# Softmax denominators of a hybrid encoder layer: from a repeated reciprocal out of PSUM to a copy, a trip through DRAM and a compact reciprocal

## Chip, cores and metric

The kernel runs on one core of a Trainium2 chip. The metric is the device time of one execution in microseconds; the time given for a kernel is the median of its runs. Engines are named as in the profile: PE is TensorE's matmul, PEld its weight load, DVE is VectorE, ACT ScalarE, POOL GpSimd, SP SyncE, which issues nearly all DMAs here.

## The reference

One encoder layer with two attention branches side by side, run on two groups of requests, 2048 and 512 tokens of width 1024. Cut to what matters:

```python
proj = h @ w_in                       # h: adaLN-modulated RMSNorm of x
qa, ka, va, za, cq, ckv, kr, zb, gm = jnp.split(proj, IN_SPLITS, axis=-1)
ya = windowed_gqa(qa, ka, va, sink) * jax.nn.silu(za)     # branch A
yb = mla(cq, ckv, kr, g_q, w_uq, g_kv, w_ukv) * jax.nn.silu(zb)   # branch B
ga, gb = jnp.split(jax.nn.sigmoid(gm), 2, axis=-1)
merged = ga * (ya @ w_oa) + gb * (yb @ w_ob)
out = x + gate_res[:, None, :] * (merged @ w_out)         # then a final RMSNorm

def attend(q_blk):                    # inside mla, 8 heads of 64 values
    s = jnp.einsum("bqhd,bkhd->bhqk", q_blk, k).astype(jnp.float32)
    p = jax.nn.softmax(s, axis=-1).astype(v.dtype)
    return jnp.einsum("bhqk,bkhd->bqhd", p, v)
```

The change concerns the division in mla's softmax: one denominator per head and token, 8 x 512 of them per chunk of 512 tokens.

## The kernel before

The 2560 tokens are five chunks of T = 512: c = 0 to 3 are the long request, c = 4 the short one. The kernel has three stages: the input projections; mla's scores, exponentials and value products; and a last stage that runs from 1311 us to the end. Every fp32 matmul of a projection is done as three passes (`mm3`, L99 to 102) over operands split into a high and a low part; each weight tile of 128x1024 is loaded by SP (`wload`, L109), its high part cast by ACT (L122) and its low part subtracted by POOL (L123).

The stage in the middle leaves, per chunk, unnormalised outputs of mla in DRAM (`o_d`) and partial sums of the exponentials over 128 partitions (`sm_d`). The last stage then does, chunk by chunk: the denominators (`inv_den`, L888 to 901), branch B's gate path (`zb(1)`, tiles z_1_0 to z_1_3), the merge gates (gm, two tiles of 24 matmuls for each of eight j) with branch B's projection (po, `branch_out`), the next chunk's `inv_den`, branch A's gate path (`zb(0)`), its projection, and the output projection (out). Branch A's windowed attention is done in groups (`attn_group`, L136 to 198, a block of 128 tokens and four heads each) set between the others.

`inv_den(c)` has two halves, b = 0 and 1. In each, PE sums the partial sums of four heads with a matmul by a matrix of ones that has 32 columns (L896), so the 512 denominators of one head stand in PSUM on 32 partitions, all alike: a 128x512 tile `den`, of which 4 rows differ. DVE inverts all of it into the SBUF tile `rd` (L899), and SP stores one row of each head to DRAM (`rd_d`, L901). `inv_den(0)` stands ahead of the loop over chunks; `inv_den(c + 1)` stands in chunk c, ahead of `zb(0)`. In `zb(1)` SP loads each head's row back, spread over 64 partitions (`dn`, L919), POOL adds the two halves of the output (`ob`, L920), and DVE multiplies by `dn` (L921). The gate path's z then goes through tanh (L928), DVE (`zt`, L929, which is what frees z's PSUM bank), POOL (L930) and a split into Y (L932, L933).

What sets the order: the middle stage's order is written out by hand; the last stage is ordered by the framework's scheduler, which works from its own simulated timeline, so a changed instruction can move others on every engine. Each engine then runs its instructions in that order. Buffers: PSUM tag "a" (den, z, gm, po, out) has four banks, used in turn, so z_1_2 takes the bank of den_0 and z_1_3 that of den_1; `rd` has one buffer in SBUF, so the second half of `inv_den` waits until the first half's rows have landed; split weights have three load buffers. SP's DMAs use eight completion semaphores in turn, so a DMA can wait for the one issued eight before it.

In `attn_group` the chain is: scores `as` (PE, L165, L166), mask and maximum (DVE, L168), `ncol` and `ecol` (DVE, L171, L172), exponentials (ACT, L173, L175), `dcol` and `rcol` (DVE, L177, L178), the scaling of S by rcol (DVE, L180), transposes `pT` (PE, L186), the split into PT (ACT L188, DVE L189), and the value product `aa` (PE, L190, L191).

```python
dn = p3.tile([P, T], F32, name=f"rd{c}_{b}", tag="rd", bufs=1)
nc.vector.reciprocal(out=dn, in_=ps)
for i in range(4):
    nc.sync.dma_start(rd_d[c][4 * b + i:4 * b + i + 1], dn[32 * i:32 * i + 1])
```

Of the kernel before, what the change touches and what calls it, by code (L numbers as in the profile page):

```python
# [9 lines left out]
F32 = mybir.dt.float32  # L10
# [8 lines left out]
P = 128  # L19
D = 1024  # L20
KD = D // P
T = 512
NS = 4
NC = 5
HA = 8
HB = 8
# [12 lines left out]
def encoder(ctx: ExitStack, tc: tile.TileContext, x_prompt, x_sample, c_prompt, c_sample, b_ada, g_norm, g_q,  # L39
            w_uq, g_kv, w_ukv, sink, g_final, t_mod, t_gate, t_col, t_a, t_b, t_oa, t_ob, t_out, rope_c, rope_s, bias, sel, y_prompt, y_sample):  # L40
    nc = tc.nc
# [12 lines left out]
    dram = ctx.enter_context(tc.tile_pool(name="dram", bufs=1, space=DRAM))  # L54
# [5 lines left out]
    def pa(name):  # L60
        return pps["a"].tile([P, 512], F32, name=name, tag="a")
# [25 lines left out]
    o_d = [dram.tile([2, HB * 64, T], F32, name=f"o_d{c}") for c in range(NC)]  # L87
    sm_d = [dram.tile([HB, P, T], F32, name=f"sm_d{c}") for c in range(NC)]
    rd_d = [dram.tile([HB, T], F32, name=f"rd_d{c}") for c in range(NC)]
    rw_d = [dram.tile([HB, 4, P], F32, name=f"rw_d{c}") for c in range(NC)]  # L90
    gate_d = dram.tile([2, D], F32, name="gate_d")
    ones_d = dram.tile([P, 1024], F32, name="ones_d")
# [13 lines left out]
    def wload(tp, nm, loads, nr, tag="wr"):  # L106
        wr = tp.tile([P, 1024], F32, name=f"wr{nm}", tag=tag, bufs=nr)
        for dst, src in loads:
            issue["w"].dma_start(dst(wr), src)  # L109
        return wr  # L110
# [749 lines left out]
    with psum("ps3a", 4) as pps["a"], psum("ps3t", 1) as pps["t"], psum("ps3c", 1) as pps["c"], pool("p3c") as p3c, pool("p3y") as p3y, pool("p3l") as p3, \  # L860
# [28 lines left out]
        def inv_den(c):  # L889
            for b in range(2):  # L890
                ps = pa(f"den{c}_{b}")
                w = [wload(p3r, f"sm{c}_{b}_{j}", [(lambda t: t.rearrange("p (h n) -> p h n", n=T),
                                                    sm_d[c][j:j + 2].rearrange("h p n -> p h n"))], NR)
                     for j in (4 * b, 4 * b + 2)]
                for i in range(4):
                    nc.tensor.matmul(ps[32 * i:32 * i + 32, :], ones, w[i // 2][:, i % 2 * T:(i % 2 + 1) * T],  # L896
                                     start=True, stop=True)
                dn = p3.tile([P, T], F32, name=f"rd{c}_{b}", tag="rd", bufs=1)
                nc.vector.reciprocal(out=dn, in_=ps)  # L899
                for i in range(4):  # L900
                    nc.sync.dma_start(rd_d[c][4 * b + i:4 * b + i + 1], dn[32 * i:32 * i + 1])  # L901

        inv_den(0)
        H = H0
        for c in range(NC):
# [64 lines left out]
            if c + 1 < NC:  # L970
                inv_den(c + 1)
# [140 lines left out]
```

## Time and profile before

| What | Value |
|---|---|
| Runs | 2640.05, 2640.7 and 2644.24 us; median 2640.7 |
| Profiled execution | 2639.86 us |
| Span of its profile, first to last instruction | 2638.1 us |
| Mean granted TensorE clock | 0.991 of full speed |
| Last stage | from about 1311 us to the end |

The rows below come from the one profiled execution. A row of a timeline gives the start in us from the span's start, the duration in us, the engine, the line, the operation with out<-in, the shape and type, a count where several are taken together, and in brackets the idle time of the engine just before and what ended it. SPq is SP issuing a DMA: its duration is the issue, not the transfer. A row of the waits gives the engine and line that waited, what it waited for, the us in total, the times and the longest. Ends of matmuls are modelled, so the pace of PE is read from starts.

### The profile page before, as it was taken

The numbers are of one execution on the slowest core, as the hardware profiler recorded it, in microseconds if no ns is written. First come the engines' busy times: TensorE is split into PE (matmuls) and PEld (weight loads), VectorE is DVE, ScalarE is ACT, GpSimd is POOL, SyncE is SP. The second block draws the span as 40 slices with busy tenths as digits, with TensorE's granted clock in tenths as the row PEclk, the third lists the DMA queues.
The fourth block names the chain that finished last, engine by engine and source line by source line (L and its number), as shares of the span: only waits on it lengthen the run. The fifth ranks groups of instructions, "written<-read, shape, count | busy, mean of one in ns | idle before, by whom it ended". The sixth has DMA issues, their size and how long they took to land. (4 is left out here: it accounts for less than half of the span.)

```text
span 2638.1 us, 33977 instructions
## 1 busy us (share of the span) xinstructions
PE 2555.9 (97%) x11842; PEld 2037.5 (77%) x11842; DVE 1689.0 (64%) x2511; ACT 1325.1 (50%) x2105; POOL 1597.4 (61%) x992
## 2 busy tenths in 40 slices
PE   7999999899999999999999999999999999999998
PEld 4888888767777777776777777877887788778876
DVE  3654644579999999999764567446644663466325
ACT  3554543367777777777644443434343434344432
POOL 2564554278888888887852376337733773377355
PEclk8999999999999999999999999999999999999999
DMA  8677765563232232222264445345544453445341
GB/s 307 217 239 239 242 214 181 154 191 92 55 96 75 60 87 75 71 68 83 80 212 161 157 167 196 121 151 174 188 135 143 165 188 124 162 150 199 107 169 53
DMA packets 199431, 392.34 MB, mean 149 GB/s; under 512 B 18086, under 2 KB 97383, under 8 KB 197658
## 3 DMA queue, kind: packets, MB, share of 16 engines
q1 hardware_dynamic: 186210, 353.32, 41.7%
q10 hardware_dynamic: 13050, 36.86, 4.4%
q8 instruction: 93, 1.52, 0.2%
q14 instruction: 78, 0.64, 0.1%
HBM read 286.52 MB, written 103.58 MB: 148 GB/s over the span
## 5 line engine op out<-in xcount | busy, mean ns | idle before, releaser
L736 POOL TENSOR_TENSOR pl<-pf,ph 128x1024 fp32r<-128x1024 f32 x272 | 655.8, 2414 | 135.6 <-ACT pf L729 135.3
L123 POOL TENSOR_TENSOR wlgm<-wrgm,whgm 128x1024 fp32r<-128x1024 f32 x80 | 196.3, 2457 | 326.5 <-ACT whgm L122 283.1
L728 ACT ACTIVATE ph<-s 128x1024 fp32r<-128x1024 f32 x272 | 278.6, 1024 | 182.2 <-PE s L721 180.7
L687 DVE TENSOR_REDUCE mx<-mp 128x1 f32<-128x1024 f32 x240 | 292.7, 1219 | 38.5 <-PE mp L681 36.7
L749 DVE TENSOR_TENSOR ac<-ac,pf 128x512 f32<-128x512 f32 x424 | 294.2, 694 | 21.3 <-ACT pf L729 14.8
L729 ACT ACTIVATE pf<-s 128x1024 f32<-128x1024 f32 x272 | 275.7, 1014 | 0.0
L101 PE MATMUL gm<-H,wlgm 128*128 128x512 f32 x640 | 252.2, 395 | 0.0
L100 PE MATMUL gm<-H,whgm 128*128 128x512 f32 x640 | 250.2, 395 | 0.9 <-ACT whgm L122 0.9
L102 PE MATMUL gm<-H,whgm 128*128 128x512 f32 x640 | 250.7, 393 | 0.0
L719 PE MATMUL s<-Q,K 97*128 97x512 f32 x544 | 216.1, 397 | 3.6 <-DMA Q<-qr_d 3.6
L720 PE MATMUL s<-Q,K 96*128 96x512 f32 x544 | 215.8, 397 | 0.0
L721 PE MATMUL s<-Q,K 96*128 96x512 f32 x544 | 215.1, 395 | 0.0
L761 PE MATMUL a<-ph,V 128*128 128x512 f32 x544 | 175.3, 403 | 0.0
L764 PE MATMUL a<-pl,V 128*64 128x512 f32 x544 | 169.7, 393 | 0.5 <-POOL pl L736 0.4
L681 PE MATMUL mp<-K,Q 96*128 96x512 f32 x512 | 163.5, 400 | 5.9 <-DVE mx L687 3.7
L123 POOL TENSOR_TENSOR wlz<-wrz,whz 128x1024 fp32r<-128x1024 f32 x39 | 95.2, 2448 | 119.5 <-ACT whz L122 112.5
L168 DVE CUSTOM_DVE_ANT_0 S<-as,mask,snk 128x384 f32<-128x384 f32 (+1 forms) x160 | 89.2, 585 | 99.4 <-PE as L166 67.3
L189 DVE TENSOR_TENSOR PT<-pT,PT 128x512 fp32r<-128x512 f32 x112 | 77.0, 688 | 110.4 <-ACT PT L188 108.8
L100 PEld LDWEIGHTS gm<-H,whgm 128*128 128x128 f32 x640 | 119.4, 188 | 26.3 <-issue 1.7
L102 PEld LDWEIGHTS gm<-H,whgm 128*128 128x128 f32 x640 | 120.4, 188 | 23.7
L101 PEld LDWEIGHTS gm<-H,wlgm 128*128 128x128 f32 x640 | 120.3, 188 | 23.4
L100 PE MATMUL z<-H,whz 128*128 128x512 f32 x320 | 127.0, 397 | 8.5 <-DVE rd L899 4.4
(254 smaller groups left out, 6487.9 us busy)
## 6 DMA issues: line engine op xcount, KB each, us to landing
wrgm<-in_t_col_dram SPq DMA_DIRECT2D x80, 512.0 KB
wrz<-in_t_col_dram SPq DMA_DIRECT2D x40, 512.0 KB
wrw<-in_t_out_dram SPq DMA_DIRECT2D x40, 512.0 KB
wrqa<-in_t_col_dram ACTq DMA_DIRECT2D x20, 512.0 KB
qa_d<-qa SPq DMA_DIRECT2D x40, 256.0 KB
k_d<-kn SPq DMA_DIRECT2D x20, 512.0 KB
qn_d<-qn SPq DMA_DIRECT2D x20, 512.0 KB
v_d<-vt SPq DMA_DIRECT2D x20, 512.0 KB
```

Source lines behind the costliest of these rows:

```text
L100: nc.tensor.matmul(ps, wh, mh, start=first, stop=False)
L101: nc.tensor.matmul(ps, wl, mh, start=False, stop=False)
L102: nc.tensor.matmul(ps, wh, ml, start=False, stop=last)
L123: (eng or nc.gpsimd).tensor_tensor(out=wl[:, :n], in0=wr[:, :n], in1=f(wh[:, :n]), op=ALU.subtract)
L687: nc.vector.tensor_reduce(out=it.mx[:, i // 2, i % 2:i % 2 + 1], in_=it.mp.rearrange("p a b -> p (a b)"), axis=AX.X, op=ALU.max)
L719: nc.tensor.matmul(ps[:, j, :], K[0:97, 0, ks], Q[0:97, 0, :], start=True, stop=False)
L720: nc.tensor.matmul(ps[:, j, :], K[0:96, 1, ks], Q[0:96, 0, :], start=False, stop=False)
L721: nc.tensor.matmul(ps[:, j, :], K[0:96, 0, ks], Q[0:96, 1, :], start=False, stop=True)
L728: nc.scalar.activation(ph, it.s, AF.Exp)
L729: nc.scalar.activation(pf, it.s, AF.Exp)
L736: nc.gpsimd.tensor_tensor(out=pl, in0=it.pf[p], in1=f(it.ph[p]), op=ALU.subtract)
L749: nc.vector.tensor_tensor(out=sm if last and j else it.acc, in0=it.acc, in1=pf[:, j], op=ALU.add)
```

## The change

ACT, not DVE, empties the PSUM tile of each half of `inv_den`: a copy into `rd` (L900 of the new kernel). SP stores the four differing rows, still not inverted, to a new DRAM buffer `dd_d` (L902). After both halves SP loads all 8 x 512 denominators of the chunk as 128 partitions by 32 columns (`dc`, L905), DVE inverts those (`rc`, L906), and SP stores them to `rd_d` (L907). The loads of `dn` are as before. Lines move by 1 after L90 and by 6 after `inv_den`: `dn` is L925 now, `ob` times `dn` L927, `zt` L935, the scaling of S L181, pT L187, the weight cast L123.

```diff
--- before.py
+++ after.py
@@ -87,6 +87,7 @@
     o_d = [dram.tile([2, HB * 64, T], F32, name=f"o_d{c}") for c in range(NC)]
     sm_d = [dram.tile([HB, P, T], F32, name=f"sm_d{c}") for c in range(NC)]
     rd_d = [dram.tile([HB, T], F32, name=f"rd_d{c}") for c in range(NC)]
+    dd_d = [dram.tile([HB, T], F32, name=f"dd_d{c}") for c in range(NC)]
     rw_d = [dram.tile([HB, 4, P], F32, name=f"rw_d{c}") for c in range(NC)]
     gate_d = dram.tile([2, D], F32, name="gate_d")
     ones_d = dram.tile([P, 1024], F32, name="ones_d")
@@ -896,9 +897,14 @@
                     nc.tensor.matmul(ps[32 * i:32 * i + 32, :], ones, w[i // 2][:, i % 2 * T:(i % 2 + 1) * T],
                                      start=True, stop=True)
                 dn = p3.tile([P, T], F32, name=f"rd{c}_{b}", tag="rd", bufs=1)
-                nc.vector.reciprocal(out=dn, in_=ps)
+                nc.scalar.copy(dn, ps)
                 for i in range(4):
-                    nc.sync.dma_start(rd_d[c][4 * b + i:4 * b + i + 1], dn[32 * i:32 * i + 1])
+                    nc.sync.dma_start(dd_d[c][4 * b + i:4 * b + i + 1], dn[32 * i:32 * i + 1])
+            dc = p3.tile([P, 32], F32, name=f"dc{c}", tag="dc", bufs=2)
+            rc = p3.tile([P, 32], F32, name=f"rc{c}", tag="dc", bufs=2)
+            nc.sync.dma_start(dc, dd_d[c].rearrange("h (a b) -> (h a) b", b=32))
+            nc.vector.reciprocal(out=rc, in_=dc)
+            nc.sync.dma_start(rd_d[c].rearrange("h (a b) -> (h a) b", b=32), rc)
 
         inv_den(0)
         H = H0
```

The order of the other instructions moves too. First SP in chunk 0, from the load of the mask on, in the order before (KA, VA and QA are the operands of branch A's groups, wrgm and wro weights):

```order
L205 DMA mask<-in_bias_dram 128x3072
L206 DMA snk<-in_sink_dram 128x8
L157 DMA KA_0_0_12529<-ka_d_111 128x2x256
L158 DMA VA_0_0_12530<-va_d_116 128x2x128
L160 DMA QA_0_0_12528<-qa_d_106 128x512
L157 DMA KA_0_1_12600<-ka_d_111 128x2x256
L158 DMA VA_0_1_12601<-va_d_116 128x2x128
L160 DMA QA_0_1_12599<-qa_d_106 128x512
L901 DMA rd_d_136<-rd_0_12501 1x512 x4
L109 DMA wrgm_0_1_13042<-in_t_col_dram 128x1024
L109 DMA wro_1_0_13073<-in_t_ob_dram 128x1024
L919 DMA dn_1_0_12746<-rd_d_136 64x512 x2
```

and the same place after the change, from the row behind snk on:

```order
L902 DMA dd_d_141<-rd_0_12506 1x512 x4
L158 DMA KA_0_0_12539<-ka_d_111 128x2x256
L159 DMA VA_0_0_12540<-va_d_116 128x2x128
L161 DMA QA_0_0_12538<-qa_d_106 128x512
L158 DMA KA_0_1_12610<-ka_d_111 128x2x256
L159 DMA VA_0_1_12611<-va_d_116 128x2x128
L902 DMA dd_d_141<-rd_1_12521 1x512 x4
L161 DMA QA_0_1_12609<-qa_d_106 128x512
L110 DMA wrgm_0_1_13052<-in_t_col_dram 128x1024
L905 DMA dc_12527<-dd_d_141 128x32
L110 DMA wro_1_0_13083<-in_t_ob_dram 128x1024
L110 DMA wrgm_1_0_13201<-in_t_col_dram 128x1024
```

The store of rc (L907) and the two loads of dn_1_0 (L925) are the next rows after these. The first half's rows went from behind the six group loads to ahead of them, and the second half's rows, which stood behind dn_1_0 and the loads of the next tile, now stand ahead of it with dc and the store of rc.

Then DVE in chunk 0, from the first reciprocal on. Before (ISA is the mask and maximum, L168):

```order
L899 RECIPROCAL rd_0_12501<-den_0_12492 128x512
L899 RECIPROCAL rd_1_12516<-den_1_12507 128x512
L929 SCALAR_TENSOR_TENSOR zt_1_0_12779<-zt_1_0_12779,z_1_0_12754 128x512
L168 ISA S_0_0_0_12537,mcol_0_0_12523<-as_0_0_0_12534,mask,snk 128x256
L168 ISA mcol_0_0_12523 128x1
L168 ISA S_0_0_1_12542,mcol_0_0_12523<-as_0_0_1_12539,mask,snk 128x256
L168 ISA mcol_0_0_12523 128x1
L921 TENSOR_TENSOR ob_1_0_12745<-ob_1_0_12745,dn_1_0_12746 128x512
L929 SCALAR_TENSOR_TENSOR zt_1_1_12826<-zt_1_1_12826,z_1_1_12795 128x512
```

and after the change:

```order
L906 RECIPROCAL rc_12528<-dc_12527 128x32
L935 SCALAR_TENSOR_TENSOR zt_1_0_12789<-zt_1_0_12789,z_1_0_12764 128x512
L169 ISA S_0_0_2_12557,mcol_0_0_12533<-as_0_0_2_12554,mask,snk 128x256
L169 ISA mcol_0_0_12533 128x1
L169 ISA S_0_0_3_12562,mcol_0_0_12533<-as_0_0_3_12559,mask,snk 128x256
L169 ISA mcol_0_0_12533 128x1
L927 TENSOR_TENSOR ob_1_0_12755<-ob_1_0_12755,dn_1_0_12756 128x512
L172 TENSOR_SCALAR ncol_0_0_12534<-mcol_0_0_12533 128x4
L173 TENSOR_TENSOR ecol_0_0_12536<-snk,mcol_0_0_12533 128x4
L178 TENSOR_TENSOR dcol_0_0_12535<-dcol_0_0_12535,ecol_0_0_12536 128x4
L179 RECIPROCAL rcol_0_0_12537<-dcol_0_0_12535 128x4
L181 TENSOR_SCALAR S_0_0_0_12547<-S_0_0_0_12547,rcol_0_0_12537 128x256
```

The first two score tiles now go through mask and maximum ahead of the reciprocal, which is one of 32 columns; the multiplication by dn_1_0 is followed at once by the softmax of group (0,0), and zt_1_1 comes behind that.

PE's order at the end of the tile gm_0_0, where group (0,0)'s transposes stand after the change:

```order
L103 MATMUL gm_0_0_13019<-H_7_11807,whgm_0_0_13022 128x512
L187 MATMUL pT_0_0_0_12578<-ident,S_0_0_0_12547 128x128
L187 MATMUL pT_0_0_0_12578<-ident,S_0_0_1_12552 128x128
L187 MATMUL pT_0_0_0_12578<-ident,S_0_0_2_12557 128x128
L187 MATMUL pT_0_0_0_12578<-ident,S_0_0_3_12562 128x128
L166 MATMUL as_0_1_2_12625<-KA_0_1_12610,QA_0_1_12609 128x256
```

Before, the four transposes stood inside the next tile, gm_0_1, behind 19 and 20 of its 24 matmuls.

## Rows read from the trace of the kernel before

**Rows 1.** The page, part 1: busy us of each engine, share, instructions.

```profile
PE 2555.9 (97%) x11842; PEld 2037.5 (77%) x11842; DVE 1689.0 (64%) x2511; ACT 1325.1 (50%) x2105; POOL 1597.4 (61%) x992
```

**Rows 2.** Windows: stretch, us; busy PE, PEld, DVE, ACT, POOL; PEclk, DMA share, GB/s.

```profile
1310.00:2638.00 1328.00, 1288.15 (x5915) 1044.69 (x5914) 707.77 (x1221) 536.92 (x1026) 697.68 (x355) 0.99 0.47 157
```

**Rows 3.** All instructions of line 899: count, ns min/median/max, first and last start.

```profile
L899 DVE RECIPROCAL rd<-den x10: 3348/3357/3358, 1319.3 to 2296.9; 128x512 f32<-128x512 f32 x10
```

**Rows 4.** PE's waits from 1300 to the end: us in total, times, longest.

```profile
PE aa L191 <- DVE PT L189: 4.8, 3, 2.6
PE z L100 <- DVE rd L899: 4.4, 1, 4.4
...
PE pT L186 <- DVE S L180: 3.9, 4, 1.6
...
PE as L165 <- DVE ecol L172: 1.4, 1, 1.4
```

**Rows 5.** PE's timeline, chunk 0: start, us, line, operation, [idle before, releaser].

```profile
1337.69 0.77 PE L100 MATMUL z<-H,whz 128*128 128x512 f32 x1 [4.43 <-DVE rd L899]
...
1342.93 0.39 PE L100 MATMUL z<-H,whz 128*128 128x512 f32 x1
...
1345.43 0.28 PE L165 MATMUL as<-KA,QA 128*128 128x256 f32 x1
...
1345.90 0.40 PE L102 MATMUL z<-H,whz 128*128 128x512 f32 x1
```

**Rows 6.** DVE's timeline, chunk 0, and scalings (L180) at 2012 us.

```profile
1334.19 3.36 DVE L899 RECIPROCAL rd<-den 128x512 f32<-128x512 f32 x1 [11.49 <-DMA rd_d<-rd]
...
1338.81 0.69 DVE L921 TENSOR_TENSOR ob<-ob,dn 128x512 f32<-128x512 f32 x1
...
1352.01 0.17 DVE L178 RECIPROCAL rcol<-dcol 128x4 f32<-128x4 f32 x1
...
1353.08 5.34 DVE L180 TENSOR_SCALAR S<-S,rcol 128x256 f32<-128x256 f32 x4
...
2011.96 1.41 DVE L180 TENSOR_SCALAR S<-S,rcol 128x384 f32<-128x384 f32 x4
```

**Rows 7.** SP's timeline, chunk 0: issues of DMAs.

```profile
1322.68 0.42 SPq L206 DMA_DIRECT2D snk<-in_sink_dram  x1
...
1328.98 2.02 SPq L901 DMA_DIRECT2D rd_d<-rd  x4
...
1333.47 1.11 SPq L919 DMA_DIRECT2D dn<-rd_d  x2
```

**Rows 8.** SP's waits from 1305 to 1350.

```profile
SPq L901 <- DMA mask<-in_bias_dram: 1.9, 1, 1.9
```

**Rows 9.** Windows: chunk 0 about the first stall, and a stall of chunk 1.

```profile
1332.00:1336.00 4.00, 1.26 (x8) 0.78 (x6) 1.81 (x1) 1.04 (x1) 0.00 (x0) 1.00 0.96 347
1337.00:1343.00 6.00, 5.31 (x13) 4.19 (x14) 4.24 (x9) 0.60 (x1) 3.77 (x3) 0.51 0.85 235
...
1623.60:1626.00 2.40, 2.40 (x13) 2.02 (x14) 1.26 (x2) 1.92 (x3) 1.69 (x2) 1.00 0.85 236
```

**Rows 10.** ACT's timeline, chunk 0.

```profile
1319.34 0.59 ACT L769 COPY o<-a 128x512 f32<-128x512 f32 x1
...
1348.34 0.50 ACT L175 ACTIVATE S<-S,ncol 128x256 f32<-128x256 f32 x1
```

**Rows 11.** PE's timeline at two other waits for DVE.

```profile
1358.48 0.33 PE L186 MATMUL pT<-ident,S 128*128 128x128 f32 x1 [0.87 <-DVE S L180]
...
1623.58 0.50 PE L191 MATMUL aa<-PT,VA 128*128 128x512 f32 x1 [2.60 <-DVE PT L189]
```

**Rows 12.** ACT's and PE's timelines, chunk 1.

```profile
1499.33 1.05 ACT L122 CAST whz<-wrz 128x1024 fp32r<-128x1024 f32 x1 [0.25 <-DMA wrz<-in_t_col_dram]
...
1500.48 0.45 PE L100 MATMUL z<-H,whz 128*128 128x512 f32 x1
```

**Rows 13.** PE's timeline, chunk 4.

```profile
2292.61 0.41 PE L165 MATMUL as<-KA,QA 128*128 128x384 f32 x1 [1.42 <-DVE ecol L172]
```

## The prediction

> **What bounds the kernel now.** I read the page first. TensorE (PE) is busy for 97% of the span and every other engine for 77% or less [rows 1], so time is won or lost only where PE stands still or runs at a lower clock. The window of the last stage says the same of the part that the change touches: 1288 of 1328 us busy at a granted clock of 0.99 [rows 2]. So a perfect last stage would save some 40 us, and less DVE work is worth only the part of it that PE waits for. Next I read all of the removed instruction: ten reciprocals of 3357 ns [rows 3], 33.6 us of DVE, yet PE's list of waits in the stage has one wait for them, 4.4 us, and a 1.4 us wait behind ecol that they may cause [rows 4]. Then I read the places themselves in the timelines. About 0.2% (5.3 us) is what a measurement of this kernel can tell from no change.
>
> The 4.43 us stall lies in chunk 0, ahead of z_1_3 [rows 5]. That tile gets den_1's PSUM bank, and the reciprocal that frees the bank waited 11.49 us for a DMA [rows 6]: tag rd has one buffer, and the first reciprocal's four rows had to land first. They were issued at 1328.98 [rows 7], after a wait of 1.9 us for the mask to land [rows 8]. After the stall twelve matmuls start in 1342.93 - 1337.69 = 5.24 us; the next eleven, from 1342.93 to 1345.43, start every 0.227 us [rows 5]. Twelve at that pace are 2.72, so the stall brought 2.5 us more. The granted clock shows why: 0.51, the level of 1.2 GHz, for six microseconds after PE stood [rows 9].
>
> **The change part by part.**
> *A. The stall on den_1.* The first copy on ACT needs what another eviction of this shape takes, 0.59 us [rows 10], and stands ahead of PE's need. The four rows of rd_0 now stand right behind snk on SP, which was issued until 1323.1; four such rows took 2.02 us [rows 7], so they are out at 1325.2. Before, a reciprocal that waited for such rows began 1334.19 - 1331.00 = 3.19 us after the last issue [rows 6, 7]. By that row copy 2 starts at 1328.4 and frees the bank at 1329.0. PE wants it at 1337.69 - 4.43 = 1333.26, 4.3 us later. The stall goes: -4.4.
> *B. The clock after it* goes with it: -2.5, given back if PE's next stall is as long.
> *C. The new chain to dn.* After copy 2 come: four rows to DRAM, load of dc, reciprocal rc, store to rd_d, load of dn, each behind the landing of the one before, on SP's one queue. SP itself went on 1333.47 - 1331.00 = 2.47 us after the rows' last issue [rows 7]; a compute engine took 3.19. The rows of rd_1 go out from 1329.0 to 1331.0; dc is issued at 1333.5, taking 0.4 as snk did [rows 7], and reaches DVE at 1337.1. The 128x32 reciprocal is not in the trace: 128x4 took 0.17 [rows 6], and 32/512 of 3.36 is 0.21, so I estimate 0.3. The store goes out by 1337.8, dn from 1340.3 to 1341.4 (1.11 for its two parts [rows 7]), and it lands at 1344.6. Before, ob x dn ran at 1338.81 [rows 6] without a wait for it.
> DVE now has ob x dn ahead of ncol, in order, so all of head group (0,0)'s softmax waits behind dn_1_0: ob 0.69, ncol taken as 0.17 like rcol [rows 6], four exponentials on ACT at 0.50 [rows 10], dcol and rcol 0.34, four scalings 1.41 [rows 6]. S is ready at 1349.2. PE is there sooner: from 1333.26 it has z_1_3 and gm_0_0, 2 x 24 x 0.227 = 10.9, and eight score matmuls, of which four took 1345.90 - 1345.43 = 0.47 [rows 5]; so it comes to pT_0_0_0 at 1345.1, and waits 4.1. Before, it waited 0.87 there [rows 11]: +3.2. Such a stall is nearly as long as the one that goes, so I charge the same clock: +2.5. A stall of 2.60 us in chunk 1 [rows 11] was followed by a granted clock of 1.00 [rows 9], so the lower bound of that part is 0. The scalings took 5.34 in one place and 1.41 in another [rows 6]; the longer one is the upper bound, +3.9 more. If dn lands early the low end of C is -0.9, PE's own 0.87 gone too.
> Against the rows stands a price from the pages: the Trainium skill (SBUF — State Buffer, section The DMA setup-cost knee) gives every DMA a roughly fixed 2 us, mostly completion. By it the five landings of the chain would cost 10.0 where the rows give 14.5, and C would be at its low end; the trace is above it in this loaded stretch.
> rc itself also stands ahead of zt_1_0 on DVE, which frees the bank that gm_0_0 takes. That would be done by 1337.4 + 0.7, and PE comes at 1333.26 + 5.9 = 1339.2: hidden, with 1.1 us to spare.
> *D. Chunk 1.* ACT's second weight cast began 0.25 us after the engine came free, and PE's z matmul at 1500.48 follows it at once, at 1499.33 + 1.05 [rows 12]. Now a copy (0.59) and an exponential (0.50) [rows 10] stand between: +1.1. Bounds 0, if the cast would wait for its weights anyway, as by 0.25 before, and 2.2, twice that. In chunks 2 to 4 I cost the copies at nothing: casts there run a tile ahead, covered by 24 x 0.227 = 5.4 us of z matmuls; without that cover each is 0.59.
> *E. Chunk 4.* A score matmul waited 1.42 for ecol [rows 13], which stood behind the chunk's two long reciprocals on DVE: -1.4, nothing if another wait takes its place.
> *F. The other reciprocals.* Eight of ten lie beside PE work and free nothing: 0; at best half of DVE's largest other claims on PE, PT 4.8 and S 3.9 [rows 4], -4.3, when DVE is emptier. In chunks 1 to 4 the chain ends far ahead of its use, since zb(0), the branch and the output projection of the chunk before lie between.
> **Sum:** -4.4 - 2.5 + 3.2 + 2.5 + 1.1 - 1.4 = -1.5. The profiled execution took 2639.86 (table of the times), so 2638.4; the median of the three runs is 0.84 above it, so **2639.2 us**. Its own range is 2635.5 to 2644, about one clock drop below and one long scaling above.
>
> **The rivals.**
> *1. The chain lands in time.* If all five landings take the shortest row's 2.47, dn is there at 1342.4 and S at 1347.0; PE stands 1.9, less than in the 2.60 stall that cost no clock, so C is +1.0 and the sum -6.2: 2634.5. If they are shorter still, the stall and the old 0.87 go: -4.4 - 2.5 - 1.4 - 0.9 + 1.1 = -8.1, and F may add to it: about 2632, down to 2628. For it: the rows of rd_0 no longer queue behind six group loads. Against it: a DMA share of 0.96 when the old rows flew and 0.85 after [rows 9]. Chance 0.34.
> *2. The in-order wait on DVE costs more than the old stall.* With 3.19 for every landing dn comes at 1346.0, and with the scalings at 5.34 S comes at 1354.5. PE stands 9.4, so 8.5 more than before, plus the clock, 2.5, and chunk 1's 2.2, against -4.4 - 2.5 - 1.4: +4.9 and, if chunk 4's wait stays, +6.3, so 2645.6 to 2647. It decides from a dn that lands after about 1345.5. For it: one long-waiting instruction (ob x dn) now stands ahead of everything that PE needs next, and rc may hold zt_1_0 as well. Against it: at 1353.08 the scalings took long only in that place. The Trainium skill (DMA: Bandwidth & Descriptors, section Specifications) says that transfers under 512 B are done as read-modify-write, and the pieces of dc and of rd_d's store have 128 B; no row here shows a price for it. Chance 0.20.
> *3. The change does not free the bank.* The rd tile still has one buffer, so copy 2 waits for a landing as reciprocal 2 did. If the rows of rd_0 wait on SP for the mask again, copy 2 comes at 1334.19 and saves only 3.36 - 0.59 = 2.8; the chain is later by as much as is left: 2638 to 2645. Chance 0.10.
>
> **How the numbers follow.** The forecast has 0.36. Faster by over 0.2% (below 2635.4): nearly all of rival 1, 0.33, and a little of the forecast, 0.02: 0.35. Slower by over 0.2% (above 2646.0): most of rival 2, 0.16, and 0.04 from the top of the forecast and of rival 3: 0.20. The rest, 0.45, lies between. The range 2629.5 to 2647.5 takes in the four cases and leaves out the far end of rivals 1 and 2, some 0.2.
>
> **What would show it.** In the timeline of chunk 0: no PE wait ahead of z_1_3 and a granted clock near 1.00 there (A, B); a copy 2 near 1328.4; rc near 1337 and ob x dn near 1344.6, with a wait on dn; a PE wait of about 4 us at pT_0_0_0 and a lower clock behind it (C). If ob x dn runs before 1342.5, rival 1 holds; if PE stands over 8 us, rival 2; if z_1_3 still waits for den_1, rival 3. In chunk 1 the second cast of z should come 1.1 us later with PE waiting for it; in chunk 4 ecol's wait should be gone. PE waits that appear in other chunks, or a reordered tail, would make the sum wrong from outside these places.

## The result, and the profile after

The changed kernel took 2660.77 us (median of 4 runs, 2657.82 to 2662.78) and the kernel before 2640.38 on the same chip (4 runs): a ratio of 1.0073, interval 1.0059 to 1.0087. It is 0.73% slower, some 20 us, where 2639.2 was forecast and 2647.5 was the top of the range. The profiled execution has a span of 2659.1 us at a mean granted clock of 0.986, against 2638.1 and 0.991.

The page of the changed kernel, part 1 (compare [rows 1]):

```profile
PE 2567.0 (97%) x11842; PEld 2043.2 (77%) x11842; DVE 1670.6 (63%) x2506; ACT 1330.1 (50%) x2115; POOL 1593.2 (60%) x992
```

The window of its last stage (columns as in [rows 2]):

```profile
1310.00:2659.00 1349.00, 1300.22 (x5921) 1050.66 (x5920) 685.47 (x1216) 543.37 (x1037) 695.03 (x356) 0.99 0.47 154
```

DVE lost 18 us of work, and the span got 21 us longer. By the two pages PE's busy time rose by 11.1 us for the same 11842 matmuls and its idle time by 9.9, so about half of the loss is matmuls that ran slower, and half is waiting. PE's waits in the last stage, changed kernel (line, what it waited for: us in total, times, longest):

```profile
PE pT L187 <- DVE S L181: 17.2, 8, 3.9
PE aa L192 <- DVE PT L190: 6.2, 4, 2.6
PE out L103 <- POOL wlw L124: 4.5, 3, 1.8
PE gm L101 <- ACT whgm L123: 2.6, 3, 1.3
PE aa L191 <- ACT PT L189: 2.2, 3, 1.0
```

The 4.4 us behind the reciprocal and the 1.4 us behind ecol of [rows 4] are no longer there, but the transposes pT wait 17.2 us for the scaled scores S where they waited 3.9.

Where in the stage the time goes is read from a **ledger**: the start of PE's n-th matmul in the changed trace minus the start of the n-th before, both from the span's start (11842 matmuls in each). Where orders differ the n-th matmul may be of another size; with each matmul weighted by its own pitch the figures move by 1 to 2 us at most places, so only larger steps are read. Each column comes from one profiled execution, and at 1305 us, ahead of everything that the change touches, the traces of the experiments already lie between -1.2 and 3.3 us.

| us before | 1305 | 1345 | 1377 | 1494 | 1504 | 1842 | 2280 | 2303 | 2440 | end |
|---|---|---|---|---|---|---|---|---|---|---|
| changed kernel, later by | 1.5 | -5.6 | 1.1 | 8.5 | 16.7 | 11.8 | 14.2 | 19.7 | 22.1 | 21.0 |

Chunk 0's stall goes, and up to 1377 us the change is about even. The loss comes in three later places: the rest of chunk 0 (1377 to 1494, +7.4), the head of chunk 1 (1494 to 1504, +8.2; weighted by pitch the two are +5.4 and +10.9), and the head of chunk 4 with its attention groups (2280 to 2440, +7.9). Some of it comes back: 4.9 us between 1504 and 1842, where the kernel before waited at 1562, 1769 and 1822 us (1.96, 1.51 and 1.55) and the changed one does not. So the new order wins waits as well as it loses them.

**Chunk 0.** ACT, DVE and PE in the timeline of the changed kernel:

```profile
1330.66 0.59 ACT L900 COPY rd<-den 128x512 f32<-128x512 f32 x1 [2.58 <-DMA dd_d<-rd]
...
1338.88 0.35 DVE L906 RECIPROCAL rc<-dc 128x32 f32<-128x32 f32 x1 [3.49 <-DMA dc<-dd_d]
...
1345.49 0.69 DVE L927 TENSOR_TENSOR ob<-ob,dn 128x512 f32<-128x512 f32 x1 [3.65 <-DMA dn<-rd_d]
...
1350.12 3.98 DVE L181 TENSOR_SCALAR S<-S,rcol 128x256 f32<-128x256 f32 x4
...
1351.28 0.47 PE L187 MATMUL pT<-ident,S 128*128 128x128 f32 x1 [3.94 <-DVE S L181]
1353.63 1.00 PE L187 MATMUL pT<-ident,S 128*128 128x128 f32 x3 [1.87 <-DVE S L181]
```

This is the forecast chain: copy, reciprocal, ob times dn (1345.49, forecast 1344.6), then PE standing for S, 5.8 us in two pieces.

**Chunk 1.** PE, DVE and POOL in the timeline of the changed kernel:

```profile
1510.55 0.50 PE L101 MATMUL z<-H,whz 128*128 128x512 f32 x1 [1.06 <-ACT whz L123]
1513.29 0.45 PE L187 MATMUL pT<-ident,S 128*128 128x128 f32 x1 [2.23 <-DVE S L181]
1515.63 0.47 PE L187 MATMUL pT<-ident,S 128*128 128x128 f32 x1 [1.89 <-DVE S L181]
1518.05 0.81 PE L187 MATMUL pT<-ident,S 128*128 128x128 f32 x2 [1.95 <-DVE S L181]
...
1510.74 7.59 DVE L181 TENSOR_SCALAR S<-S,rcol 128x384 f32<-128x384 f32 x4
...
1510.58 7.21 POOL L124 TENSOR_TENSOR wlz<-wrz,whz 128x1024 fp32r<-128x1024 f32 x3 [23.55 <-ACT whz L123]
```

and the head of chunk 1 in the kernel before, DVE and POOL:

```profile
1502.57 3.36 DVE L899 RECIPROCAL rd<-den 128x512 f32<-128x512 f32 x1 [0.61 <-DMA rd_d<-rd]
...
1507.31 1.41 DVE L180 TENSOR_SCALAR S<-S,rcol 128x384 f32<-128x384 f32 x4
...
1499.15 4.76 POOL L123 TENSOR_TENSOR wlz<-wrz,whz 128x1024 fp32r<-128x1024 f32 x2 [20.28 <-ACT whz L122]
1504.38 2.40 POOL L123 TENSOR_TENSOR wlz<-wrz,whz 128x1024 fp32r<-128x1024 f32 x1 [0.47 <-ACT whz L122]
```

After the change the four transposes stand behind one z matmul, at place 821 of the stage's order on PE (counted in the tables that hold the orders in the second set below). In the kernel before, the same four stand at place 966, among the matmuls po, and wait for nothing (PE):

```profile
1534.84 0.60 PE L186 MATMUL pT<-ident,S 128*128 128x128 f32 x4
```

So the new order has pulled this group 145 places forward, to where its S is not ready. And the four scalings that it needs run beside POOL's subtractions, the first three ending shortly after one each: 7.59 us for the four, where four of this form without POOL took 1.41. At this head before, scalings (of another group) began after 1506.8, when POOL had finished; the long reciprocal had run beside POOL at its usual 3.36. Windows of the changed kernel over the two stalls (columns as in [rows 9]) give the clock at about half, 1.2 GHz:

```profile
1351.00:1357.00 6.00, 3.84 (x11) 2.81 (x12) 6.00 (x12) 0.84 (x2) 2.63 (x3) 0.52 0.48 163
...
1511.00:1521.00 10.00, 3.92 (x11) 2.68 (x11) 9.59 (x11) 4.95 (x12) 6.69 (x3) 0.53 1.00 339
```

**Chunk 4.** PE, DVE and POOL in the timeline of the changed kernel:

```profile
2304.83 0.45 PE L187 MATMUL pT<-ident,S 128*128 128x128 f32 x1 [3.26 <-DVE S L181]
...
2302.13 1.81 DVE L172 TENSOR_SCALAR ncol<-mcol 128x4 f32<-128x4 f32 x1
...
2301.58 2.34 POOL L124 TENSOR_TENSOR wlz<-wrz,whz 128x1024 fp32r<-128x1024 f32 x1 [17.75 <-PE as L167]
```

Again transposes at the head of a z tile; here a small DVE operation, ncol, stood 1.81 us beside POOL.

So there were three suspects: the order that the scheduler now made, the collision of DVE's scalings with POOL, and the new chain itself.

### The profile page after: what moved, and what is told of

It is laid out like the page before. It is cut to its first block, busy times and chain, and to the rows that moved or that the text cites. A ratio compares the mean times of both kernels' runs of the same rounds, so it can differ in the third digit from the quotient of the medians.

```text
span 2659.1 us, 33994 instructions
## 1 busy us (share of the span) xinstructions
PE 2567.0 (97%) x11842; PEld 2043.2 (77%) x11842; DVE 1670.6 (63%) x2506; ACT 1330.1 (50%) x2115; POOL 1593.2 (60%) x992
## 5 line engine op out<-in xcount | busy, mean ns | idle before, releaser
L953 DVE SCALAR_TENSOR_TENSOR G<-G,po 128x512 f32<-128x512 f32 x80 | 53.4, 683 | 142.1 <-PE po L103 86.2
L190 DVE TENSOR_TENSOR PT<-pT,PT 128x512 fp32r<-128x512 f32 x112 | 77.0, 688 | 99.6 <-ACT PT L189 98.3
```

## The experiments

Ratios are to the kernel before on the same chip. The columns behind the ratio are the ledger, "End" its last entry.

| Kernel | Median us (before) | Ratio, interval | 1305 | 1377 | 1494 | 1504 | 2280 | 2303 | End |
|---|---|---|---|---|---|---|---|---|---|
| changed kernel | 2660.77 (2640.38) | 1.0073, 1.0059 to 1.0087 | 1.5 | 1.1 | 8.5 | 16.7 | 14.2 | 19.7 | 21.0 |
| copy, no trip | 2648.05 (2644.17) | 1.0018, 1.0009 to 1.0028 | 1.7 | 2.0 | 4.8 | 5.0 | 4.2 | 8.7 | 10.4 |
| trip, long reciprocal | 2650.04 (2644.17) | 1.0029, 1.0018 to 1.0041 | 2.2 | 8.5 | 10.3 | 12.4 | 9.0 | 13.1 | 13.3 |
| changed, scaling on ACT | 2658.03 (2644.17) | 1.0057, 1.0040 to 1.0074 | 1.0 | -1.0 | 4.3 | 4.3 | 13.3 | 16.9 | 17.3 |
| before, scaling on ACT | 2652.24 (2644.17) | 1.0036, 1.0023 to 1.0049 | -1.2 | -4.1 | -3.9 | -3.1 | 5.8 | 8.9 | 7.9 |
| new in old order | 2652.19 (2643.27) | 1.0036, 1.0024 to 1.0049 | 0.2 | 6.3 | 6.3 | 8.5 | 9.4 | 10.2 | 10.7 |
| old in new order | 2665.36 (2643.27) | 1.0081, 1.0066 to 1.0096 | -0.4 | -0.9 | 8.0 | 15.9 | 17.4 | 26.2 | 27.6 |
| new order, scaling on ACT | 2662.30 (2643.27) | 1.0069, 1.0054 to 1.0084 | 1.8 | 0.3 | 7.8 | 12.6 | 11.4 | 19.2 | 22.6 |
| copy, no trip, old order | 2648.16 (2643.27) | 1.0022, 1.0010 to 1.0034 | 2.8 | 6.5 | 6.5 | 9.5 | 9.7 | 11.9 | 12.0 |
| new order, pT later | 2659.73 (2641.92) | 1.0067, 1.0050 to 1.0084 | 3.3 | 5.3 | 12.7 | 18.4 | 14.9 | 18.4 | 19.8 |
| old order, waits shifted | 2639.46 (2641.92) | 0.9993, 0.9984 to 1.0003 | 0.2 | 0.2 | 0.2 | 0.4 | -0.8 | -0.8 | -1.4 |
| new in old order, chunk 0 old | 2644.27 (2641.92) | 1.0009, 1.0000 to 1.0019 | 0.8 | 1.0 | 1.0 | 1.8 | 0.9 | 0.8 | 2.5 |
| new order, pT and z later | 2653.89 (2642.34) | 1.0042, 1.0027 to 1.0056 | 1.0 | 1.0 | 8.4 | 13.1 | 11.8 | 13.7 | 14.4 |

### First set: one part at a time, order left to the scheduler

*Copy, no trip*: ACT empties PSUM, rows go straight to rd_d, and nothing is inverted. The diffs of this set are against the changed kernel, or, for *before, scaling on ACT*, against the kernel before.

```diff
-                    nc.sync.dma_start(dd_d[c][4 * b + i:4 * b + i + 1], dn[32 * i:32 * i + 1])
-            dc = p3.tile([P, 32], F32, name=f"dc{c}", tag="dc", bufs=2)
...
-            nc.sync.dma_start(rd_d[c].rearrange("h (a b) -> (h a) b", b=32), rc)
+                    nc.sync.dma_start(rd_d[c][4 * b + i:4 * b + i + 1], dn[32 * i:32 * i + 1])
```

> The new kernel without the trip: ACT's copy goes straight to rd_d, dc and rc are gone (the inversion is left out, so mla is multiplied by the denominators). Theory 1 (the removed reciprocal held DVE back; the softmax scalings of S now run beside POOL's weight subtractions, each as long as one of those, 2.4 us, and the transposes wait): the order round chunk 4's denominators is that of the new kernel, so a wait of about 3 us for S and its clock stay there (+5); in chunk 1 the transposes that stood behind the first z matmul are those of an older group, so chunk 1's +10 goes: 2642 to 2652 in all. Theory 2 (the two DRAM hops make dn and rc late on DVE, and all else follows): dn is there at once, no wait for S in chunks 0, 1 and 4: at or under 2640.

*Trip, long reciprocal*: the 128x512 reciprocal stays on DVE, and the trip is added (what it brings back is inverted a second time).

```diff
-                nc.scalar.copy(dn, ps)
+                nc.vector.reciprocal(out=dn, in_=ps)
```

> The new kernel with DVE's 128x512 reciprocal in place of ACT's copy, the trip and the compact reciprocal kept (inverted twice, so mla is multiplied by the denominators). Theory 1: DVE is held as before, the scalings in chunks 1 and 4 come after POOL's subtractions, and the +10 and +5 there go; chunk 0 has reciprocal and trip in series and loses 5 to 15: 2645 to 2656. Theory 2: the trip is all, so at least as slow as the new kernel, 2660 or more.

*Changed, scaling on ACT* and *before, scaling on ACT*, to take the scalings off the engine that collides with POOL:

```diff
-            nc.vector.tensor_scalar(out=Ss[i][:, 0:kw], in0=Ss[i][:, 0:kw], scalar1=rcol[:, i:i + 1], scalar2=None,
-                                    op0=ALU.mult)
+            nc.scalar.activation(Ss[i][:, 0:kw], Ss[i][:, 0:kw], AF.Copy, scale=rcol[:, i:i + 1])
```

> The new kernel with the four scalings of S per head group on ACT (a copy with a scale per partition) and nothing else changed in the source. Theory 1: no scaling can be held by POOL, the 6 us wait in chunk 1 and the 3 us wait in chunk 4 shrink to under 1.5, and the kernel is at 2640 or below (to 2632), ACT having room at 50% busy. Theory 2: chunk 0 and the rest as in the new kernel, 2655 or more.

> The kernel before with the four scalings of S per head group on ACT. Theory 1: the kernel before has only some 4 us of PE waits for S and 5 for PT, so it gains 0 to 6: 2634 to 2641; if the new kernel with the same edit comes to the same time, the scalings were the difference. Theory 2: this one stays near 2640 and the other stays 15 or more above it.

Measured: all four were slower than before, by 0.18 to 0.57%, and each lost its time in other places. The copy alone lost 4.5 us at chunk 4's head, where it has no trip. The trip alone lost 6.3 us in chunk 0 up to 1377 us, 2.1 in chunk 1 and 4.1 at chunk 4's head, which theory 1 had gone. The times of these two are those that theory 1 (the collision) gave, but the third kernel is its test: with scaling on ACT chunk 1 lost nothing, 4.9 us appeared between 1842 and 1900 us, and the time was 2658 where theory 1 wanted 2640 or less. As the explanation of the whole loss it fell. With the scalings on ACT in both kernels the changed one is 5.8 us behind instead of 20.4; whether the scalings or yet another order closed the gap, these two runs can't tell. None of the four was a clean test, since the scheduler ordered each anew: in the changed kernel, 4381 of the 5848 matmuls of the stage stand at another place in PE's order than before.

### Second set: instructions and order apart

For this the order of the instructions that both kernels share in the last stage was held, on all five engines, by ordering dependencies without semaphores, from a table taken from the other kernel (`c` lists the shared instructions, ORDER is the table):

```diff
+    for row in ORDER:
+        for a, b in zip(row, row[1:]):
+            tc.add_manual_dep(c[b], c[a].name, info, reason="order")
```

*New in old order* has the changed kernel's instructions in the order of before; *old in new order* is the reverse.

> The new kernel, with all instructions of the last stage that both kernels have held in the order of the kernel before, engine by engine; the copies, the rows' stores, dc, rc and its store stand where the scheduler puts them. Theory A (the 20 us come from the new order that the scheduler makes, not from the new instructions): no wait for S in chunks 1 and 4, the 4.4 us wait of chunk 0 gone or replaced by one of 2 to 6 behind the late dn, so 2634 to 2643, within 6 us of the kernel before. Theory B (copies and trip cost the time themselves): 15 us or more above the kernel before.

> The reverse: the kernel before, its reciprocals out of PSUM and no trip, with all other instructions of the last stage in the order of the new kernel. Theory A: the order alone costs most of it, 10 to 25 us above the kernel before. Theory B: without copies and trip it is as fast as the kernel before, within 5 us.

Measured: the old instructions in the new order lost 0.81% (22 us, as theory A had it), as much as the change itself; the new ones in the old order lost 0.36%, half of it, and the intervals of the two don't overlap. **The new order loses the time in the three places, with either set of instructions, and the old order takes most of it away there.** From 1377 to 1494 us the ledger has +7.4 in the changed kernel, +8.9 with the old instructions in the new order, and 0.0 with the new ones in the old order; at chunk 1's head +8.2, +7.9 and +2.2; at chunk 4's head (2280 to 2303) +5.5, +8.8 and +0.8. The 0.81% isn't the order's share in the changed kernel, though: part of these waits stands behind the long reciprocals, which the changed kernel no longer has. The old instructions' PE and DVE rows in chunk 1, from the timeline:

```profile
1516.71 1.37 PE L186 MATMUL pT<-ident,S 128*128 128x128 f32 x4 [4.75 <-DVE S L180]
...
1511.95 3.35 DVE L900 RECIPROCAL rd<-den 128x512 f32<-128x512 f32 x1
...
1516.14 1.41 DVE L180 TENSOR_SCALAR S<-S,rcol 128x384 f32<-128x384 f32 x4
```

The same transposes wait, but here for scalings that stand behind a long reciprocal and meet no POOL work. So the place of the transposes makes the wait, and whatever delays S (a collision, a reciprocal) sizes it.

The loss of the new instructions in the old order lies mostly in chunk 0 (+6.3 of 10.7 by 1377 us). It is above the 6 us that theory A allowed and below the 15 of theory B. Its DVE and PE rows there:

```profile
1343.57 0.69 DVE L928 TENSOR_TENSOR ob<-ob,dn 128x512 f32<-128x512 f32 x1 [3.81 <-DMA dn<-rd_d]
...
1357.55 5.24 DVE L181 TENSOR_SCALAR S<-S,rcol 128x256 f32<-128x256 f32 x4
...
1349.15 0.39 PE L166 MATMUL as<-KA,QA 128*128 128x256 f32 x1 [4.06 <-DVE mcol L169]
...
1362.84 0.48 PE L187 MATMUL pT<-ident,S 128*128 128x128 f32 x1 [1.87 <-DVE S L181]
```

The stall on den_1 is gone (the ledger is at -7.1 by 1345 us), DVE stands 3.81 us for dn, PE then 4.06 us for DVE, and 13.4 us are given back by 1377.

*New order, scaling on ACT* holds the changed kernel's order and moves only the scalings, by the edit above. *Copy, no trip, old order* is the first kernel of the first set (no inversion) in the order of before.

> The new kernel with its own order held and only the four scalings of S per group moved to ACT, where POOL can't hold them. If the collision of the scalings with POOL's weight subtractions is what makes the waits for S in chunk 1 (6.1 us and its clock) and chunk 4, the wait in chunk 1 falls to some 3 us, and the kernel gains 5 to 12 of its 20 us. If the collision is not the cause, it stays within 4 us of the new kernel.

> The kernel with ACT's copy and no trip (the inversion is left out, the denominators go to rd_d as they are), in the order of the kernel before. Theory A with a cheap trip: the same as the new kernel in the old order within 3 us. If the trip costs by itself in chunk 0, through DVE's in-order wait for dn: 3 to 8 us faster than that one, and 5 to 9 us faster than the kernel before, since the 4.4 us stall and its clock go and nothing takes their place.

Measured: with the order held and the scalings on ACT, PE's waits for S at chunk 1's head fell from 6.1 to 2.6 us and the step there from 8.2 to 4.8, so the collision with POOL sizes about 3 us of it. The 5 to 12 us that were to be gained did not come: the whole run was not faster, 1.0069 against 1.0073, intervals overlapping, and chunk 4's head lost 7.8 instead of 5.5. By their forms, DVE's scalings in the changed kernel and ACT's in this one (group | busy us, mean ns | idle before):

```profile
L181 DVE TENSOR_SCALAR S<-S,rcol 128x384 f32<-128x384 f32 x128 | 75.6, 652 | 1.1
```

```profile
L181 ACT ACTIVATE S<-S,rcol 128x384 f32<-128x384 f32 x128 | 68.4, 607 | 10.7 <-DVE rcol L179 10.6
```

On DVE they take 652 ns in the mean, collisions included, and on ACT 607: little to win. Without the trip, the kernel in the old order took 2648.16 us against 2652.19 with it, 4 us less with intervals that overlap, and was still above the kernel before. By 1377 us it was as late (+6.5 against +6.3), but its trace began 2.8 us late at 1305, so it lost 3.7 us in chunk 0 against 6.1. Its DVE row:

```profile
1344.23 0.69 DVE L922 TENSOR_TENSOR ob<-ob,dn 128x512 f32<-128x512 f32 x1 [6.74 <-DMA dn<-rd_d]
```

So the two more legs of the trip are at most a part of the loss there, some 2 us in these traces, and dn is late in that order without them. What makes it late was not settled: the loads of dn were issued at 1336.68, 3.2 us later than in [rows 7], but this trace runs some 3 us late there as a whole, and their rows came to DVE only at 1344.23.

### Third set: single places

*New in old order, chunk 0 old*: chunks 1 to 4 get the new path, chunk 0 keeps the reciprocal out of PSUM.

```diff
+                if c == 0:
+                    nc.vector.reciprocal(out=dn, in_=ps)
...
+                    continue
+            if c == 0:
+                return
```

> The changed kernel in the order of the kernel before, and for chunk 0 alone with the old inversion of 128 by 512 out of PSUM; chunks 1 to 4 keep the copy, the trip through DRAM and the small reciprocal. In that order with all five chunks changed the loss was 0.36%, of which +6 us stood by 1377 us, in chunk 0. Theory (in a held order chunks 1 to 4 cost next to nothing, chunk 0 carries the loss): the first 180 us of the stage as before, +0 to +1.5, and the end +2 to +6, ratio 1.0005 to 1.0025. Rival (the loss is spread: the trip's DMAs and the copies slow every chunk): end +7 or more, ratio above 1.003.

Measured: 1.0009 (1.0000 to 1.0019), end +2.5. That is what the first theory expected. In the old order, the copies, the trips and the small reciprocals of four chunks cost about 2 us, and chunk 0's new path some 7 more (0.36% less 0.09%).

*New order, pT later*, *new order, pT and z later*: in the changed kernel's order of PE, first two groups of four transposes moved, then one matmul more.

```diff
 z_0_0 H_0,whz
-pT_1_0_0 x4
-z_0_1 H_0,whz
 z_0_0 x14
+pT_1_0_0 x4
 z_0_0 x9
+z_0_1 H_0,whz
...
-pT_4_0_0 x1
 z_3_0 H_0,whz
-pT_4_0_0 x3
 z_3_0 x7
+pT_4_0_0 x4
```

The two rows on z_0_1 are the second kernel's alone. In chunk 4 the transposes stand behind 8 z matmuls, not 9.

> The changed kernel with the order of all engines held as it is, but on PE two groups of four transposes later: pT1_0_0_0 stands behind 15 z matmuls instead of behind 1, and pT4_0_0_0 behind 9 instead of around 1. Theory (the loss of chunks 1 and 4 comes from transposes that stand ahead of matmuls that could run, and PE waits there for S): in chunk 1 some 6 us of waits fall to about 2 to 3 (the low halves of the z weights are ready only about 1513 us, so not to nothing), in chunk 4 3.3 us fall to below 1; with the clock kept the kernel gains 5 to 12 us on the changed one, ratio to before about 1.003 to 1.0055; the step from 1494 to 1504 us falls from +8.2 to about +3 or +4. Rival (the DVE chain of mask, exponential and scaling is what is late, wherever its reader stands): the gain is given back at the matmuls aa that follow, and the time stays within 3 us of the changed kernel, ratio 1.006 to 1.0085.

> As the kernel with the two groups of transposes later, and one matmul more: the first one of z_0_0_1, which stood between the transposes and the rest of z_0_0_0 and there waited 3.70 us for the second cast of weights on ACT (behind exponentials, which waited for DVE, whose small operation stood 2.2 us beside a subtraction of POOL), now stands behind all 24 matmuls of z_0_0_0. Theory (chunk 1 is lost by the place of a few instructions on PE): PE then has 14 z matmuls to run while S is scaled, the step from 1494 to 1527 us falls from +6.0 in the run before and +8.8 in the changed kernel to +1 to +3, and the end is 3 to 5 us earlier than in the run before, ratio to before about 1.004 to 1.006. Rival (the supply is late: the low half of z_0_0_0 comes only some 6 us behind the scores, and the groups of scores that filled that time in the kernel before have been computed earlier): PE waits for the low half in place of the cast, the step stays at +5 or more and the ratio at 1.006 to 1.008.

Measured: the first gained nothing that can be told (1.0067 against 1.0073), as its rival had it. PE met the next instruction that wasn't ready; PE and DVE in its timeline:

```profile
1518.54 0.79 PE L101 MATMUL z<-H,whz 128*128 128x512 f32 x1 [3.70 <-ACT whz L123]
...
1514.51 2.22 DVE L178 TENSOR_TENSOR dcol<-dcol,ecol 128x4 f32<-128x4 f32 x1
```

The first matmul of z_0_1 needed a cast that stood on ACT behind an exponential, which waited for DVE. With that one moved too, the ratio came to 1.0042, an interval clear of the changed kernel's: 11.6 us over before instead of 20.4, for nine matmuls in other places. Its PE rows in chunk 1:

```profile
1510.72 0.50 PE L101 MATMUL z<-H,whz 128*128 128x512 f32 x1 [1.40 <-ACT whz L123]
1513.24 0.79 PE L102 MATMUL z<-H,wlz 128*128 128x512 f32 x1 [2.02 <-POOL wlz L124]
```

Three waits for S, 6.1 us, became one of 2.0 for POOL. The step from 1494 to 1527 us fell from 8.8 to 4.8: less than expected (1 to 3), so a wait for the low half of the weights remains, as the rival said. Chunk 4's step fell from 5.5 to 1.9. The time is what the first theory expected.

*Old order, waits shifted*: the kernel before, with five places where PE waited, among them the 2.60 us of [rows 11] and the 1.42 us of [rows 13], moved behind 2 to 6 matmuls that can run.

```diff
-aa_1_0_0 x1, pT_1_0_0 x4
 out_0_0_0 x4
+aa_1_0_0 x1, pT_1_0_0 x4
...
-as_4_1_1 x4
 z_3_0 x4
+as_4_1_1 x4
```

> The kernel before with its instructions and order held, but on PE five places altered where it waits in chunks 1 and 4: matmuls aa and transposes pT of the attention groups stand 4 to 6 matmuls (in chunk 4 5 scores and 2 to 5) later, behind matmuls that can run. Their waits of 1.96, 1.65, 2.60, 1.42 and 0.91 us sum to 8.5 us. Theory (place in PE's order alone carries microseconds, with no instruction changed): 3 to 8 us faster than before, ratio 0.997 to 0.999. Rival (a wait removed comes back at the next place, as it did in chunk 0 of the changed kernel): within 3 us of before, ratio 0.999 to 1.001.

Measured: 0.9993 (0.9984 to 1.0003), no difference that can be told, and not the 3 to 8 us of the first theory. Two of the five waits shrank (1.65 to 0.33, 0.91 to none). Three stayed (1.96 to 1.95, 2.60 to 2.37, and 1.42 for ecol came back as 1.25 for the low half of z's weights at the next matmul), as the rival said. So a later place does not end every wait. The run also serves as a control: from 1377 to 1504 us, ahead of its first shift at about 1553 us, its ledger stands at 0.2 to 0.4, so an order held by hand cost nothing there. It is no faster version, and none of the twelve runs beat the kernel before.

## Why the prediction was wrong, by its steps

- **A and B, right.** The wait on den_1 is gone and so is the lower clock behind it (1.00 from 1330 to 1345 us). From 1305 to 1345 us the ledger goes from +1.5 to -5.6, -7.1 against a forecast of -6.9. Copy 2 came at 1330.66, 2.3 us later than worked out; the 4.3 us to spare covered it.
- **C, right in place and chain, size close.** Forecast +5.7; from 1345 to 1377 the ledger gives back 6.7. PE stood 5.8 us instead of 4.1, because two of the scalings were long. From the end of the second copy (1331.25) to ob times dn took 14.2 us, against 15.6 from the rows. That span has four landings; the five that the prediction counts include the one ahead of copy 2. With the roughly fixed 2 us a DMA of the Trainium skill (SBUF — State Buffer, section The DMA setup-cost knee) an estimate for the span is 12.3 (15.6 less 11.3 for the four by the rows, plus 8.0); the trace is nearer the rows.
- **D, failed.** The step priced chunk 1 by a weight cast that comes 0.59 + 0.50 us later: +1.1, at most 2.2. It measured +8.2. The cast does come late (a wait of 1.06), but the price is in the four transposes that the new order puts behind the first z matmul, 145 places earlier than before: 6.1 us of waits for S, and the lower clock with them.
- **E, right in part and wrong in sum.** The wait for ecol went (-1.4), and a wait of 3.26 us for S took its place at a transpose nearby; with what follows, chunk 4's head came to +5.5. "Nothing if another wait takes its place" named the event, and priced it too low.
- **F, failed, and this is the main error.** Eight reciprocals, and the chunks in which they lie, were charged 0 because PE didn't wait for them. But taking them away gave every engine another order. That order costs 0.81% with the old instructions in it, and going back to the old order takes half of the changed kernel's loss away. The rest of chunk 0 (+7.4) and chunk 4's groups (+4.6 from 2395 to 2440) had no term at all, and neither had the 4.9 us that came back between 1504 and 1842. The working compared the two orders at chunk 0 and stopped there.
- **The rivals.** None was this mechanism. Rival 2, DVE's in-order wait, priced 2645.6 to 2647 and looked at chunk 0, where the forecast held. The last sentence of the prediction (waits in other chunks, a reordered tail) was the case that came, without a price or a chance.

Order and instructions don't add up: 22 us for the order alone, 9 for the instructions alone, 20 for both (differences of the medians in the table). In the new order the new path costs nothing more, as the changed kernel stands no worse than the old instructions in that order. Order and path compete for the same waits.

Open: between 1377 and 1494 us of the kernel before (+7.4) PE stands for 3.1 us in the changed kernel (busy 120.92 of 124.00 from 1377 to 1501) and not at all in the kernel before (117.00 of 117.00), at a granted clock of 1.00 in both; the larger waits are 1.03 (for PT) and 1.33 (for whgm). The order makes the loss, since it is 0.0 in the old order, but not one place that I could name. Also open is what makes dn late in chunk 0 in the old order. Why the scheduler chose this order was not tried either.

## What to carry to other kernels

Where a scheduler orders the code, an edit is two changes: the instructions and the order that follows from them. Compare the orders over the whole stage, look for short dependent work (here transposes) that now stands ahead of long ready work, and test the two apart by holding the order. With PE busy for 97% of the span, removing 18 us of another engine's work was worth only the waits that it ended, and a wait that goes may uncover the next one in the same place.

## What the runs showed of the hardware that was not expected

Some VectorE operations on SBUF that met GpSimd's subtractions were seen to end only with them or just after: in the changed kernel's last stage all ten scalings, and all nine ncol, that began inside a subtraction with time left to end in it. Four scalings took 7.59 us beside three subtractions and 1.41 without, and a 128x4 addition took 2.22 us where the same operation took 0.16 elsewhere. Not every operation was held: a reciprocal out of PSUM in the same company took its usual 3.36, PT (L190), which reads PSUM, its usual 0.69, and the compact reciprocal, from SBUF to SBUF, 0.35 in chunk 4 (at 2311.13) as in chunk 0. Over the stage the scalings went from 73.4 us before to 89.7 (all forms of the line summed; the larger form, before):

```profile
L180 DVE TENSOR_SCALAR S<-S,rcol 128x384 f32<-128x384 f32 x128 | 57.9, 513 | 1.1
```

against 75.6 for the same 128 in the changed kernel. Stalls cost more than they last: with waits of 5.8 us in chunk 0 and 6.1 us in chunk 1 the granted clock was 0.52 over the 6 us and 0.53 over the 10 us of the windows shown above, and the matmuls behind them started slower until it rose. Length alone did not decide it: the stall of 2.60 us in [rows 11] was followed by a clock of 1.00, and one of 2.61 us at 1638.17 in the changed kernel by 0.50 (1638 to 1641 us).
